# One ring tile for the split weights, with a fixed place for stationary operands, and a fourth buffer for raw weights

## The chip, the cores and the metric

The kernel runs on one core of a Trainium2 chip. The metric is device time in microseconds (us) of one execution. The kernel before took 2450.12 us, the median of 3 runs (2442.09 to 2450.7).

## The reference

One layer of a streaming encoder over 256 tokens of width 2048, in float32. Four sub-layers follow each other, each as x += post(f(pre(x))) with RMS norms:

```python
h = rmsnorm(x, n_ffn1_pre)                       # 1. SwiGLU FFN, 2048 -> 5504 -> 2048
x = x + 0.5 * rmsnorm((silu(h @ w_gate) * (h @ w_up)) @ w_down, n_ffn1_post)
proj = rmsnorm(x, n_mix_pre) @ w_in              # 2. two token mixers, gated
merged = gates[0] * mla_branch(proj) + gates[1] * rwkv7_branch(proj)
x = x + rmsnorm(merged @ w_o, n_mix_post)
x = x + rmsnorm(memory_xattn(rmsnorm(x, n_x_pre), mem), n_x_post)   # 3. over 256 memory tokens
# 4. a second SwiGLU FFN, as 1
```

Nearly all arithmetic is in products of the 256 token rows with float32 weight matrices, 437 MB of reads in all.

## The kernel before

**Split products.** TensorE multiplies float32 in a reduced format (float32r). So each operand is split into a high part, which is the value cast to that format, and a low part, the remainder, and a product is three products: high by high, high by low, low by high. For activations the two parts are tiles such as `hT` (the normed input, transposed; 16 blocks of 2048 bytes per partition, each with 256 high and 256 low elements), `mh` and `ml` (the FFN's hidden values), `oT`, `mT`, `zh`, `zl`. For weights they are made on the fly.

**Weight tiles.** All weights go through `weights` (L156 to L182), in tiles of up to 128 x 1024 elements (512 KB, laid out in memory so that one transfer brings one tile). Per tile: SP issues the load into a raw buffer (`wraw`, L176), ScalarE casts it into the high part (`whi`, L178), VectorE subtracts (`wlo`, L179), TensorE reads both. `wraw`, `whi` and `wlo` are pools of three buffers each. A raw buffer is free again when VectorE has read it; a `whi` buffer when TensorE's last matmul on it is done.

**Two kinds of product.** `lin_ch` (L188) makes channel-major results. The weights are the stationary operand, loaded into TensorE 128 columns at a time, and `hT` streams through: L196 multiplies a block of `whi` with the high and low half of `hT` at once (512 columns), L199 a block of `wlo` with the high half (256 columns). One tile of 1024 weight columns serves eight such pairs. `lin_tok` (L209) makes token-major results. The activations are stationary and the weights stream: L217 (high by `whi`), L218 (high by `wlo`), L219 (low by `whi`).

**Where the tiles lie.** In `lin_ch` the tile is not at the start of its buffer: a counter `turn` shifts it by (L165)

```python
a, b = 32 * (self.turn % 4), 32 * (self.turn // 4 % 4)
```

elements of 4 bytes, `a` in `whi` and `b` in `wlo`. In `lin_tok` both are 0. The buffers are 4608 bytes apart (9 x 512), and as built, `hT` starts at byte 50688 of each partition, the first `whi` buffer at 95744 and the first `wlo` buffer at 109568; each is a multiple of 512 bytes away from `hT`.

**Which product comes when.** Tiles in the order of the code: FFN1 gate and up (172, `lin_ch`), w_down (88, `lin_tok`), the latents of w_in (14, `lin_tok`), the low-rank columns of w_in (4, `lin_ch`), the v columns (16, `lin_tok`), w_ukv and w_uq (12, `lin_tok`), r and k columns of the first head group (16, `lin_ch`), w_oa (16, `lin_tok`), r and k of the second group (16, `lin_ch`), the gates (64), w_ob (16) and w_o (32, all `lin_tok`), then w_ckv in turns of 4 `lin_ch` and 4 `lin_tok` tiles, three times; four `lin_ch` products with w_cq (16); the fourth turn of w_ckv (4 and 4); w_co (16, `lin_tok`); FFN2 as FFN1.

**Feeds.** For FFN1 and for the memory tokens, `hT` itself is made from a raw buffer: `feed` (L335 to L340) loads a transposed block of x or mem (`in_xT`, `in_memT`) into a `wraw` buffer and splits it. There the three raw buffers hold activations and weights by turns. In FFN1's first column group the gate and up products advance in step, four blocks of `hT` at a time. x itself is loaded after the last split of the feed (L1113), for the row norms; their reciprocal roots are spread over a tile by L259.

**Order of the work.** A scheduler in the tile library orders the instructions of each engine by the order of the code and by priorities (the casts stand 100 places ahead, L177), and sets the waits between engines from the bytes that each instruction reads and writes. Every engine works its own list in order.

Of the kernel before, what the change touches and what calls it, by code (L numbers as in the profile page):

```python
# [18 lines left out]
P = 128  # L19
# [5 lines left out]
KF = DFF // P  # L25
EPS = 1e-6
WT = 1024
SKEW = 4
LEAD = 100

# [46 lines left out]
class Layer:  # L77
    def __init__(self, ctx, tc, a):
        self.ctx, self.tc, self.nc, self.a = ctx, tc, tc.nc, a
        nc = self.nc  # L80
        mk = lambda n, b, **k: ctx.enter_context(tc.tile_pool(name=n, bufs=b, **k))
        self.const = mk("const", 1)
        self.hpool = mk("hpool", 2)
        self.dram = mk("dram", 1, space=bass.MemoryType.DRAM)
        self.wraw = mk("wraw", 3)
        self.whi = mk("whi", 3)
        self.wlo = mk("wlo", 3)
        self.tmp = mk("tmp", 1)
        self.stat = mk("stat", 4)
        self.gp = mk("gp", 2)  # L90
        self.psm = mk("psm", 4, space=PSUM)
        self.pst = mk("pst", 2, space=PSUM)
        self.pss = mk("pss", 2, space=PSUM)

        self.ident = self.const.tile([P, P], F32, tag="ident", name="ident")
        make_identity(nc, self.ident)
        self.cols = self.const.tile([P, NCOL], F32, tag="cols", name="cols")
        nc.scalar.dma_start(out=self.cols, in_=a["cols"])
        self.inv = self.const.tile([P, 32], F32, tag="inv", name="inv")
        nc.scalar.dma_start(out=self.inv, in_=a["inv"])  # L100
        self.mhalf = self.const.tile([P, 1], F32, tag="mhalf", name="mhalf")
        nc.gpsimd.memset(self.mhalf, -0.5)

        self.pad(self.const, 128)
        warm = self.const.tile([P, 1], F32, tag="warm", name="warm")
        nc.scalar.activation(out=warm, in_=self.mhalf, func=AF.Copy, scale=self.mhalf)
        self.pad(self.gp, 64)
        self.lead = LEAD
        self.turn = 0
        self.X = self.hpool.tile([P, NT, D], F32, tag="big", name="X")  # L110

    def pad(self, pool, n):
# [43 lines left out]
    def weights(self, w, nk, c0, n, feed=None, still=False):  # L156
# [3 lines left out]
        for k in range(0, nk, kt):  # L160
            m = min(kt, nk - k)
            raw = self.wraw.tile([P, WT], F32, tag="wraw", name="wraw")
            a = b = 0
            if still:
                a, b = 32 * (self.turn % 4), 32 * (self.turn // 4 % 4)  # L165
                self.turn += 1
            hi = self.whi.tile([P, WT + 128], F32R, tag="whi", name="whi")[:, a : a + WT]
            lo = self.wlo.tile([P, WT + 128], F32R, tag="wlo", name="wlo")[:, b : b + WT]
            o = P * (nk * c0 + k * n)
            src = w[o : o + P * m * n].rearrange("(p x) -> p x", p=P)  # L170
            step = 1 if k == 0 and feed is not None else m
            for j in range(0, m, step):
                if feed is not None:
                    feed(k + j, step)
                e = slice(j * n, (j + step) * n)
                nc.sync.dma_start(out=raw[:, e], in_=src[:, e])  # L176
                with self.ahead(self.lead):  # L177
                    nc.scalar.copy(out=hi[:, e], in_=raw[:, e])  # L178
                    self.last_split = nc.vector.tensor_sub(  # L179
                        out=lo[:, e], in0=raw[:, e], in1=hi[:, e].bitcast(F32))  # L180
                for i in range(j, j + step):
                    yield k + i, hi[:, i * n : (i + 1) * n], lo[:, i * n : (i + 1) * n]  # L182
# [1021 lines left out]
```

## Time and profile before

| | before |
|---|---|
| median of 3 runs | 2450.12 us (2442.09 to 2450.7) |
| the profiled execution | 2451.06 us |
| its span, first to last instruction | 2449.3 us |
| mean granted TensorE clock | 0.99 |
| TensorE busy (PE) | 2391.3 us, 98% |
| VectorE busy (DVE) | 1489.7 us, 61% |
| ScalarE busy (ACT) | 1146.5 us, 47% |
| DMA | 450.36 MB, 184 GB/s |

PE is TensorE's matmul side, PEld its loading of stationary operands, which overlaps with PE. Busy times are between an instruction's modelled start and end, and matmuls overlap each other, so how fast TensorE goes is read from the starts of successive matmuls. SPq is SP's queue, which issues the loads.

### The profile page before, as it was taken

The page shows a single profiled execution, that of the slowest core. Times are in us where ns is not written, and L with a number is a line of the kernel's source. Part 1 is how long each engine was busy: PE and PEld are TensorE (multiplying, and loading weights), DVE is VectorE, ACT ScalarE, POOL GpSimd, SP SyncE. Part 2 cuts the span into 40 slices and gives each one's busy share as a digit, 9 for nine tenths or more (in the row PEclk, how much of TensorE's full clock was granted, in tenths as well). Part 3 has the DMA queues.
Part 4 walks back from the last instruction along what each step waited for, and adds up shares of the span by engine and source line. Part 5 has one row for each costly group of instructions (what it writes and reads, how often), then busy time and mean ns, then how long its engine had stood idle before and what let it go on. Part 6 is the DMA issues. An engine that isn't in the chain of part 4 may idle for free.

```text
span 2449.3 us, 33193 instructions
## 1 busy us (share of the span) xinstructions
PE 2391.3 (98%) x12682; PEld 2023.3 (83%) x12682; DVE 1489.7 (61%) x2262; ACT 1146.5 (47%) x1700; POOL 88.1 (4%) x126
## 2 busy tenths in 40 slices
PE   8999999999999999999999999999999999999997
PEld 6888888888888877887877677987888888888886
DVE  5666666654447566774873757555666666664444
ACT  6444444444446455443432446445554444444443
POOL 0000000000000102002011100000000000000000
PEclk9999999999999999999999999999999999999999
DMA  6555555556666644453653676545455555565664
GB/s 229 193 187 187 188 188 189 189 194 198 198 195 208 208 145 138 147 179 99 182 190 120 205 247 200 187 147 189 162 187 188 187 189 189 189 197 188 203 197 152
DMA packets 138719, 450.36 MB, mean 184 GB/s; under 512 B 24000, under 2 KB 26560, under 8 KB 138304
## 3 DMA queue, kind: packets, MB, share of 16 engines
q1 hardware_dynamic: 132896, 434.17, 54.6%
q0 software_dynamic: 4944, 13.64, 1.9%
q8 instruction: 99, 1.62, 0.3%
q10 hardware_dynamic: 720, 0.44, 0.1%
q14 instruction: 60, 0.49, 0.1%
HBM read 437.69 MB, written 10.49 MB: 183 GB/s over the span
## 4 chain that ended last, share of the span: by engine, by line
PE 87%; DMA 4%; DVE 4%; issue 2%; ACT 2%; POOL 1%; SPq 0%; DVEq 0%; ACTq 0%; POOLq 0%
PE mm L196 30%; PE mm L199 16%; PE mm L219 12%; PE mm L218 11%; PE mm L217 11%; DVE wlo L179 2%; PE po L847 1%; ACT whi L178 1%; PE po L848 1%; PE gr L802 1%; PE pn L860 1%; DMA ov<-osc 0%; DMA wraw<-in_xT 0%; PE po L869 0%; DMA wraw<-in_w_o 0%
## 5 line engine op out<-in xcount | busy, mean ns | idle before, releaser
L179 DVE TENSOR_TENSOR wlo<-wraw,whi 128x1024 fp32r<-128x1024 f32 (+2 forms) x796 | 960.1, 1207 | 724.1 <-ACT whi L178 715.6
L178 ACT CAST whi<-wraw 128x1024 fp32r<-128x1024 f32 (+2 forms) x796 | 826.1, 1038 | 921.2 <-PE mm L219 448.2
L196 PE MATMUL mm<-hT,whi 128*128 128x512 f32 x3296 | 1159.4, 396 | 8.1 <-DVE hT L288 5.6
L199 PE MATMUL mm<-hT,wlo 128*128 128x256 f32 x3296 | 916.1, 284 | 3.1 <-DVE wlo L179 3.1
L196 PEld LDWEIGHTS mm<-hT,whi 128*128 128x128 f32 x3296 | 615.5, 189 | 143.4 <-ACT whi L178 9.2
L199 PEld LDWEIGHTS mm<-hT,wlo 128*128 128x128 f32 x3296 | 622.9, 189 | 18.5 <-DVE wlo L179 6.4
L219 PE MATMUL mm<-whi,ml 128*128 128x512 f32 x688 | 267.7, 389 | 0.0
L218 PE MATMUL mm<-wlo,mh 128*128 128x512 f32 x688 | 267.7, 389 | 0.0
L217 PE MATMUL mm<-whi,mh 128*128 128x512 f32 x688 | 267.6, 389 | 0.0
L218 PE MATMUL mm<-wlo,hT 128*128 128x512 f32 (+2 forms) x512 | 187.4, 366 | 2.7 <-DVE wlo L179 2.7
L217 PE MATMUL mm<-whi,hT 128*128 128x512 f32 (+2 forms) x512 | 187.5, 366 | 0.5 <-ACT hT L287 0.5
L219 PE MATMUL mm<-whi,hT 128*128 128x512 f32 (+2 forms) x512 | 187.6, 367 | 0.0
L218 PEld LDWEIGHTS mm<-wlo,mh 128*128 128x128 f32 x688 | 129.1, 188 | 27.1
L217 PEld LDWEIGHTS mm<-whi,mh 128*128 128x128 f32 x688 | 129.1, 188 | 26.9
L219 PEld LDWEIGHTS mm<-whi,ml 128*128 128x128 f32 x688 | 129.1, 188 | 26.4
L205 ACT COPY half<-mm 128x256 f32<-128x256 f32 x206 | 75.6, 368 | 141.7 <-PE mm L196 141.7
L206 DVE TENSOR_TENSOR half<-half,mm 128x256 f32<-128x256 f32 x206 | 85.7, 417 | 56.9 <-ACT half L205 56.9
L218 PEld LDWEIGHTS mm<-wlo,hT 128*128 128x128 f32 x512 | 97.4, 190 | 18.1 <-DVE wlo L179 4.0
L217 PEld LDWEIGHTS mm<-whi,hT 128*128 128x128 f32 x512 | 97.4, 190 | 14.7 <-ACT hT L287 0.8
L219 PEld LDWEIGHTS mm<-whi,hT 128*128 128x128 f32 x512 | 97.0, 190 | 14.8 <-issue 1.0
L251 POOL TENSOR_TENSOR rstd<-rstd,mhalf 128x1 f32<-128x1 f32 x22 | 14.1, 644 | 1827.9 <-DVE rstd L249 1791.3
L218 PE MATMUL mm<-wlo,mT 128*128 128x512 f32 x128 | 50.8, 397 | 0.5 <-DVE wlo L179 0.5
(276 smaller groups left out, 1900.4 us busy)
## 6 DMA issues: line engine op xcount, KB each, us to landing
wraw<-in_w_ffn_up SPq DMA_DIRECT2D x172, 512.0 KB, 4.1
wraw<-in_w_ffn_gate SPq DMA_DIRECT2D x171, 512.0 KB, 4.2
wraw<-in_w_ffn_down SPq DMA_DIRECT2D x168, 512.0 KB, 4.2
wraw<-in_w_in SPq DMA_DIRECT2D x124, 512.0 KB, 3.4
wraw<-in_w_o SPq DMA_DIRECT2D x32, 512.0 KB, 3.3
wraw<-in_w_ckv SPq DMA_DIRECT2D x31, 512.0 KB, 3.4
wraw<-in_w_oa SPq DMA_DIRECT2D x16, 512.0 KB, 3.3
wraw<-in_w_ob SPq DMA_DIRECT2D x16, 512.0 KB, 4.7
```

Of the source, the lines that this page charges most:

```text
L178: nc.scalar.copy(out=hi[:, e], in_=raw[:, e])
L179: self.last_split = nc.vector.tensor_sub(out=lo[:, e], in0=raw[:, e], in1=hi[:, e].bitcast(F32))
L196: both = lambda: nc.tensor.matmul(ps[j], hi[:, s], x[:, k], start=(k == 0), stop=(k == nk - 1))
L199: nc.tensor.matmul(ps[j][:, 0, :], lo[:, s], x[:, k, 0], start=False, stop=False)
L205: nc.scalar.copy(out=y, in_=ps[j][:, 1, :])
L206: nc.vector.tensor_add(y, y, ps[j][:, 0, :])
L217: nc.tensor.matmul(ps[t], xh[:, k, s], hi, start=(k == 0), stop=False)
L218: nc.tensor.matmul(ps[t], xh[:, k, s], lo, start=False, stop=False)
L219: self.last_mm = nc.tensor.matmul(ps[t], xl[:, k, s], hi, start=False, stop=(k == nk - 1))
L802: nc.tensor.matmul(ps[:, p, :], self.bk[:, c, p, :], self.ar[:, c, p, :], start=True, stop=True)
L847: nc.tensor.matmul(po[:, p, :], self.ar[:, c, p, :], S[:, p, :], start=(p == 0), stop=False)
L848: nc.tensor.matmul(po[:64, p, :], G[64:, c, p, :64], self.uv[64:, c, p, :], start=(S is None and p == 0), stop=(p == GP - 1))
```

## The change

The two pools of three buffers for the split weights become one tile each, `whi` and `wlo`, used as a ring of three slots of 1024 elements. `turn` now counts every weight tile, modulo 3, and picks the slot. In `lin_ch` a tile lies at a fixed 64 elements (256 bytes) past the start of its slot in `whi` and 32 elements (128 bytes) in `wlo`; in `lin_tok` at the start of the slot. So a `lin_ch` tile reaches 64 (32) elements into the slot behind; behind the third slot these elements are spare. The raw weights get four buffers instead of three. The pools of scratch tiles stand in another order, and as built `whi` lies at byte 123904 and `wlo` at 99840, with `hT` at 50688 as before; xattn's own `hT` at 136704. Lines below L27 move down by two, lines between the constructor and `weights` by four, those behind L168 by one.

```diff
 WT = 1024
+RING = 3
+STILL = (64, 32)
 SKEW = 4
...
-        self.wraw = mk("wraw", 3)
-        self.whi = mk("whi", 3)
-        self.wlo = mk("wlo", 3)
+        self.wraw = mk("wraw", 4)
+        self.lo_pool = mk("lo", 1)
+        self.stat = mk("stat", 4)
         self.tmp = mk("tmp", 1)
-        self.stat = mk("stat", 4)
         self.gp = mk("gp", 2)
+        self.hi_pool = mk("hi", 1)
...
-        self.pad(self.gp, 64)
         self.lead = LEAD
         self.turn = 0
+        self.whi = self.hi_pool.tile([P, RING * WT + STILL[0]], F32R, tag="whi", name="whi")
+        self.pad(self.hi_pool, 512 - 4 * STILL[0])
+        self.wlo = self.lo_pool.tile([P, RING * WT + STILL[1]], F32R, tag="wlo", name="wlo")
...
             raw = self.wraw.tile([P, WT], F32, tag="wraw", name="wraw")
-            a = b = 0
-            if still:
-                a, b = 32 * (self.turn % 4), 32 * (self.turn // 4 % 4)
-                self.turn += 1
-            hi = self.whi.tile([P, WT + 128], F32R, tag="whi", name="whi")[:, a : a + WT]
-            lo = self.wlo.tile([P, WT + 128], F32R, tag="wlo", name="wlo")[:, b : b + WT]
+            a, b = (WT * self.turn + x for x in (STILL if still else (0, 0)))
+            self.turn = (self.turn + 1) % RING
+            hi, lo = self.whi[:, a : a + WT], self.wlo[:, b : b + WT]
```

The same instructions run, on all engines; some stand elsewhere in their engine's list. ScalarE where FFN1 passes from w_up to w_down, in the kernel before (4607 is the raw buffer of the last tile of w_up, 4642 of the first of w_down, 4660 of its second; the names in brackets are the semaphores waited for):

```order
L178 CAST whi_4608<-wraw_4607 128x1024 [waits DMAHW3_49,PE_49,Activation_49]
L284 CAST mh_110<-sg_4426 128x256 [waits DVE_49]
L178 CAST whi_4643<-wraw_4642 128x1024 [waits DMAHW4_49,PE_49,Activation_49]
L205 COPY half_4577<-mm_4532 128x256
L178 CAST whi_4661<-wraw_4660 128x1024 [waits DMAHW5_49,PE_49,Activation_49]
L404 ACTIVATE sg_4580<-sg_4580 128x256 [waits DVE_49]
```

and there in the changed kernel (4267 is the last tile of w_up, 4300 the first of w_down, 4316 and 4332 its second and third):

```order
L179 CAST whi_104<-wraw_4267 128x1024 [waits DMAHW3_49,PE_49,Activation_49]
L285 CAST mh_112<-sg_4100 128x256 [waits DVE_49]
L206 COPY half_4239<-mm_4198 128x256 [waits PE_49]
L405 ACTIVATE sg_4242<-sg_4242 128x256 [waits DVE_49]
L179 CAST whi_104<-wraw_4316 128x1024 [waits DMAHW5_49,PE_49,Activation_49]
L179 CAST whi_104<-wraw_4300 128x1024 [waits DMAHW4_49,PE_49,Activation_49]
L179 CAST whi_104<-wraw_4332 128x1024 [waits DMAHW6_49]
```

The cast of w_down's first tile moved behind that of its second, and both behind the copies of the product before. TensorE at the same place, before:

```order
L199 MATMUL mm<-hT,wlo 128x256 x2
L196 MATMUL mm<-hT,whi 128x512
L217 MATMUL mm<-whi,mh 128x512 [waits Activation_49]
L218 MATMUL mm<-wlo,mh 128x512 [waits DVE_49]
L219 MATMUL mm<-whi,ml 128x512
L217 MATMUL mm<-whi,mh 128x512 [waits PE_49]
```

and in the changed kernel, there and, after the dots, at the first w_ckv product of the memory tokens:

```order
L200 MATMUL mm<-hT,wlo 128x256 x2
L197 MATMUL mm<-hT,whi 128x512
L218 MATMUL mm<-whi,mh 128x512 [waits Activation_49]
L218 MATMUL mm<-whi,mh 128x512 [waits PE_49]
L219 MATMUL mm<-wlo,mh 128x512 [waits DVE_49]
L220 MATMUL mm<-whi,ml 128x512
...
L318 MATMUL tr<-ident,X 128x128 x7
L218 MATMUL mm<-whi,hT 128x256 x2
L219 MATMUL mm<-wlo,hT 128x256
L220 MATMUL mm<-whi,hT 128x256
```

Two products with the high part now stand ahead of the first with the low part, and at w_ckv seven transposes ahead of both; before, that product followed its `lin_ch` directly. SP's list at the kernel's start, before:

```order
L337 DMA wraw<-in_xT 128x256
L176 DMA wraw<-in_w_ffn_gate 128x256 x3
L337 DMA wraw<-in_xT 128x256 [waits DMAHW1_49,DMAHW0_49,DVE_49]
L337 DMA wraw<-in_xT 128x256 [waits DMAHW4_49,DVE_49]
L176 DMA wraw<-in_w_ffn_up 128x1024 [waits DMAHW5_49,DMAHW6_49,DMAHW3_49,DMAHW7_49,DMAHW2_49,DVE_49]
```

and in the changed kernel:

```order
L338 DMA wraw<-in_xT 128x256
L177 DMA wraw<-in_w_ffn_gate 128x256
L338 DMA wraw<-in_xT 128x256
L177 DMA wraw<-in_w_ffn_gate 128x256
L177 DMA wraw<-in_w_ffn_gate 128x256 [waits DMAHW0_49]
L338 DMA wraw<-in_xT 128x256 [waits DMAHW1_49,DVE_49]
L177 DMA wraw<-in_w_ffn_up 128x1024 [waits DMAHW4_49,DMAHW2_49,DVE_49]
```

A third load of `in_xT` now stands among the gate's, without a wait for VectorE.

## Rows read from the trace of the kernel before

**Rows 1.** The page: busy times of the engines; the chain that ended last, by engine.

```profile
PE 2391.3 (98%) x12682; PEld 2023.3 (83%) x12682; DVE 1489.7 (61%) x2262; ACT 1146.5 (47%) x1700; POOL 88.1 (4%) x126
...
PE 87%; DMA 4%; DVE 4%; issue 2%; ACT 2%; POOL 1%; SPq 0%; DVEq 0%; ACTq 0%; POOLq 0%
```

**Rows 2.** Groups by shape, matmuls: count, busy us, mean ns; idle time before.

```profile
L196 PE MATMUL mm<-hT,whi 128*128 128x512 f32 x3296 | 1159.4, 396 | 8.1 <-DVE hT L288 5.6 <-ACT whi L178 1.9 <-DVE half L206 0.5
...
L199 PE MATMUL mm<-hT,wlo 128*128 128x256 f32 x3296 | 916.1, 284 | 3.1 <-DVE wlo L179 3.1
...
L217 PE MATMUL mm<-whi,mh 128*128 128x512 f32 x688 | 267.6, 389 | 0.0
```

**Rows 3.** Windows, L196 alone: stretch, length, PE (count), PEld (count), clock, DMA.

```profile
0.00:291.00 291.00, 275.46 (x777) 146.30 (x777) 0.99 0.60 198
```

**Rows 4.** Timeline of PE (start us, length): first matmuls of still tiles.

```profile
291.00 0.39 PE L196 MATMUL mm<-hT,whi 128*128 128x512 f32 x1
...
305.00 0.39 PE L196 MATMUL mm<-hT,whi 128*128 128x512 f32 x1
...
307.78 0.39 PE L196 MATMUL mm<-hT,whi 128*128 128x512 f32 x1
...
335.78 0.39 PE L196 MATMUL mm<-hT,whi 128*128 128x512 f32 x1
...
349.79 0.39 PE L196 MATMUL mm<-hT,whi 128*128 128x512 f32 x1
...
352.56 0.39 PE L196 MATMUL mm<-hT,whi 128*128 128x512 f32 x1
```

**Rows 5.** Groups by shape, the split of a weight tile on VectorE and ScalarE.

```profile
L179 DVE TENSOR_TENSOR wlo<-wraw,whi 128x1024 fp32r<-128x1024 f32 x766 | 937.6, 1224 | 705.2 <-ACT whi L178 696.7
...
L178 ACT CAST whi<-wraw 128x1024 fp32r<-128x1024 f32 x766 | 806.0, 1052 | 897.2 <-PE mm L219 430.8 <-PE mm L196 257.9 <-issue 148.9
```

**Rows 6.** Timeline near 11 and 592 us; in brackets idle time and releaser.

```profile
10.68 1.05 ACT L178 CAST whi<-wraw 128x1024 fp32r<-128x1024 f32 x1 [1.80 <-DMA wraw<-in_w_ffn_up]
...
11.78 0.50 PEld L196 LDWEIGHTS mm<-hT,whi 128*128 128x128 f32 x2 [1.19 <-ACT whi L178]
...
13.04 0.29 PEld L199 LDWEIGHTS mm<-hT,wlo 128*128 128x128 f32 x1 [0.76 <-DVE wlo L179]
...
591.69 0.39 PE L218 MATMUL mm<-wlo,mh 128*128 128x512 f32 x1
591.92 0.39 PE L219 MATMUL mm<-whi,ml 128*128 128x512 f32 x1
...
592.35 1.06 ACT L178 CAST whi<-wraw 128x1024 fp32r<-128x1024 f32 x1 [1.66 <-PE mm L219]
```

**Rows 7.** Windows around two waits of TensorE: PE, PEld, DVE, ACT, POOL, clock, DMA.

```profile
1338.00:1350.00 12.00, 10.42 (x41) 7.25 (x40) 7.78 (x12) 4.99 (x6) 2.02 (x2) 1.00 0.64 218
...
1380.00:1392.00 12.00, 10.00 (x42) 7.84 (x41) 7.95 (x11) 4.33 (x5) 0.00 (x0) 0.86 0.62 212
```

**Rows 8.** The start: window, two xT loads in SP's timeline, one wait of TensorE.

```profile
0.00:32.00 32.00, 25.74 (x111) 19.88 (x112) 16.69 (x27) 17.24 (x30) 0.74 (x7) 1.00 0.68 221
...
7.91 0.33 SPq L337 DMA_DIRECT2D wraw<-in_xT  x1
...
21.27 0.33 SPq L337 DMA_DIRECT2D wraw<-in_xT  x1
...
PE rB L259 <- POOL rstd L251: 3.5, 1, 3.5
```

**Rows 9.** The feed of memT: window, and one wait of ScalarE (total, times, longest).

```profile
1500.00:1522.00 22.00, 18.59 (x99) 14.83 (x98) 20.52 (x39) 17.47 (x41) 1.10 (x2) 1.00 0.68 226
...
ACT hT L287 <- DMA wraw<-in_memT: 2.8, 3, 1.0
```

## The prediction

> **What bounds the kernel now.** I read four views: the page, the groups by shape, the timeline of TensorE, the waits. The page shows TensorE busy for 2391.3 of 2449.3 us, and the chain that ended last lies on it for 87% [rows 1]. VectorE and ScalarE have slack, so only two things can move the end: the distance from one matmul's start to the next, and the places where TensorE waits. Of its matmuls, 3296 pairs have weights as the stationary operand (L196 with whi over 512 columns, L199 with wlo over 256); the others (L217 to L219) stream the weights [rows 2]. Each weight tile serves eight such pairs, so there are 3296 / 8 = 412 of these tiles ("still" tiles), and `turn` counts them from 0.
>
> **The offset term.** In the kernel before, tile number t lies 128 x (t % 4) bytes (whi) and 128 x (t // 4 % 4) bytes (wlo) past hT's place modulo 512, so its trace already holds all 16 combinations. The change keeps one of them, 256 and 128, which is t % 16 = 6. By 291.00 us, 776 matmuls of L196 have started and the 777th starts [rows 3], so tile 97 begins there. Tile 113 begins at 335.78: sixteen tiles, all combinations once, take 44.78 us, 2.799 each. Tile 102 (t % 16 = 6) takes 307.78 - 305.00 = 2.78 us, and tile 118, also 6, takes 352.56 - 349.79 = 2.77 us [rows 4]. No wait lies in these stretches. So a pair costs 349.8 ns on average and 346.9 ns at 256 and 128. Saving: 2.799 - 2.775 = 0.024 us a tile, times 412 = **-9.9 us**. Rounding of the starts (0.01 us) leaves -7 to -13. That this place is reached follows from the built addresses: hT at byte 50688 of a partition, whi at 123904, wlo at 99840, both a multiple of 512 from hT; xattn's own hT, at 136704, too. The streamed tiles had offset 0 and keep it, so L217 to L219 get no term.
>
> These rows say that the place of a stationary operand costs time. The Trainium skill says the opposite: SBUF — State Buffer, section "Who interferes with whom", gives PE two read ports, one for the moving operand and one for LDWEIGHTS, "independent", and has PE never wait on anyone. This case's trace disagrees (2.799 against 2.775 us); by the rule the term would be nil and the sum +2.2 us, which is a rival below.
>
> **The hand-over term.** A ring of three slots of 1024 elements takes the place of three separate buffers. A still tile in slot r ends 64 elements (32 in wlo) inside slot r + 1. When the next tile is a streamed one, at offset 0, its cast writes these elements, so it must wait until TensorE has read the last still tile whole. Before, it waited for the tile three back. This is a new wait. The order shows it: in the first FFN the cast of the second w_down tile now stands ahead of that of the first, which waits on PE, and TensorE takes both hi products (L218) before the first lo product (L219). Tiles counted in the order of the code, the product changes from lin_ch to lin_tok after 172, 278, 322, 354, 470, 478, 486, 510 and 702 tiles. The slot is this number modulo 3; slot 0 is clear of it, because slot 2's tail lies in the spare elements behind the ring. That leaves five places: 172 (w_down of FFN1), 278 (v projection), 322 (w_oa), 470 and 478 (w_ckv).
>
> Price of one: a cast of 1024 takes 1052 ns and its subtraction 1224 ns [rows 5]. The cast starts 592.35 - 591.92 = 0.43 us after the start of the last matmul that it waits for, and where TensorE waited for a fresh tile in the start phase, the load of the lo operand came 13.04 - 10.68 = 2.36 us after the cast's start [rows 6]. So the first lo matmul starts 2.79 us after the last still matmul instead of three places later (3 x 0.23 = 0.69): 2.1 us. At 172, 278 and 322 nothing longer than two small transposes stands between, and I take 2.1 each. At 470 and 478 seven or more transposes of 128 columns do (the order shows them at 470): 0 to 2.1 each. I take half, since seven of them are about as long as one of the two pieces that the wait is made of. Sum 3 x 2.1 + 2 x 1.05 = **+8.4 us**, bounds 4 and 10.5. Queued behind the waiting cast on ScalarE are the next cast and the copies of the last lin_ch result; they would have waited for the same matmuls anyway.
>
> A halved clock could follow. With 1.6 us of idle TensorE in 12 us around 1343 the granted clock stayed 1.00; with 2.0 us idle around 1385 it was 0.86, 28% of 12 us at 1.2 instead of 2.4 GHz, so 1.7 us lost [rows 7]. The new idle time comes in two pieces of about 1.3 and 0.8 us, so it is nearer to the first row, and I take nothing; the bound is three times 1.7 = 5 us.
>
> **The fourth raw buffer.** In steady state ScalarE waits for TensorE to free whi, not for weights, so nothing is gained there. It matters where hT itself is built from raw buffers. At the start, loads of xT are issued at 7.91 and, two further on, at 21.27: 6.7 us for a group of three buffers (xT, gate, up), each released by VectorE before the next load [rows 8]. TensorE's work on a group is 16 pairs x 0.35 = 5.6 us. With four buffers the same latency gives 6.7 x 3/4 = 5.0 us, under 5.6, so TensorE sets the pace: 1.1 us saved in each of three groups. The third xT load now stands ahead of two gate pieces on SP's queue and no longer waits for VectorE, so the first up tile finds its buffer sooner; TensorE's weight load waited 1.19 us for that tile's cast [rows 6], of which I count 0.9. Sum 3 x 1.1 + 0.9 = **-4.2 us**. Bounds: 0, if transfers share the same rate; -6.3, all TensorE time not busy in the first 32 us (32 - 25.74). The wait for the row of rstd behind it (3.5 us, L259 [rows 8]) moves with it, since x is loaded after the last split of the feed.
>
> The feed of memT in xattn is the same thing once more: TensorE is idle for 22 - 18.59 = 3.4 us there, and ScalarE waits 2.8 us for memT [rows 9]. I take -2, bounds 0 and -3.4.
>
> **Edits that I cost at nothing.** The pools stat, tmp and gp move; only VectorE, ScalarE and GpSimd touch them, and their waits are covered by TensorE's 98%. Without that cover, L179's own idle time would have to be gone first. The scheduler's other reorderings are swaps of near neighbours; I allow 3 us either way in the range.
>
> **Sum.** -9.9 + 8.4 - 4.2 - 2 = -7.7 us. Against the profiled execution's 2451.06 us (span 2449.3) that is 2443.4; the median of the runs shown, 2450.12, is 0.9 below that execution, so the forecast for a median is 2442.4 us.
>
> **Rivals.**
> 1. *The hand-overs are hidden.* The cast may start sooner than its place in ScalarE's order says, or the fourth buffer fills the time. For it: at two places transposes already stand between. Against it: the cast's wait on PE is in the order, and a cast and a subtraction in series have a measured length. Then -9.9 - 4.2 - 2 = -16.1: 2434 us. Chance 0.22.
> 2. *The fourth buffer gives nothing.* At the start the 16 DMA engines are busy 0.68 of the time [rows 8], and more transfers in flight could each take longer. Then -9.9 + 8.4 = -1.5: 2448.6 us. Chance 0.20.
> 3. *Slower: the hand-over costs the clock as well.* Mechanism: TensorE idles at the five places, and its clock falls to half after each. Price 2.1 + 1.7 = 3.8 us each, 19 us in all, with the offset term kept and the buffer term lost: -9.9 + 19 = +9.1, 2459 us. It decides once a hand-over costs over (9.9 + 6.2) / 5 = 3.2 us with the buffer term, 2.0 without. Against it: the row at 1343 [rows 7]. Chance 0.08.
> 4. *The place of the operand costs nothing after all*, the difference between tiles having another cause. Then 8.4 - 6.2 = +2.2: 2452.3 us. The two tiles that agree speak against it [rows 4]. Chance 0.03. It is what the page SBUF — State Buffer of the Trainium skill would have.
>
> **How the numbers follow.** The forecast has 0.47. Its own range, from the bounds of its terms, is 2436 to 2450. A measurement of this kernel cannot tell changes under 0.5%, 12.3 us, from none: faster means under 2437.9, slower over 2462.4. Rival 1 lies mostly under it (0.16 of 0.22), and the forecast's lower tail adds 0.09: faster 0.25. Slower: half of rival 3 and a rest, 0.05. Same 0.70. For 8 in 10 the range takes in rival 2 and most of rival 1, and leaves out the ends of 1 and 3: 2433 to 2455.
>
> **What will show it.** In the timeline every still tile without a wait takes 2.77 to 2.78 us; if tiles still differ, the offset term is wrong. TensorE shows a wait of about 1.3 us for whi and then 0.8 us for wlo at the first w_down, v and w_oa products; if not, rival 1. The granted clock stays 1.00 there; if not, rival 3. At the start xT loads follow at 5.6 us instead of 6.7, and the row of rstd comes about 4 us earlier; if they do not, rival 2.

## The result, and the profile after

The changed kernel took 2435.64 us, the median of 16 runs (2428.35 to 2445.38), against 2450.45 us for the kernel before in 16 runs beside it. The ratio is 0.9944, with a 95% interval of 0.9928 to 0.9960, so about 14 us less. A second set of four runs (below) gave 2428.82 us and 0.9908 (0.9894 to 0.9923). The forecast was 2442.4 us, the range 2433 to 2455. Both kernels vary by some 8 us either way from run to run; most of it is clock, as shown below.

The profiled execution of the changed kernel took 2441.6 us, with a span of 2439.8 us, at a mean granted clock of 0.986 (before: 2451.06 us at 0.990). In the lines shown here every line number is one higher than before. First the page's busy times and the chain that ended last, which answer to [rows 1]:

```profile
PE 2385.9 (98%) x12682; PEld 2021.7 (83%) x12682; DVE 1487.9 (61%) x2262; ACT 1144.7 (47%) x1700; POOL 85.9 (4%) x126
...
PE 91%; DVE 4%; DMA 2%; issue 1%; ACT 1%; POOL 1%; SPq 0%; DVEq 0%; ACTq 0%; POOLq 0%
```

The chain now lies on TensorE for 91% instead of 87%, and on DMA for 2% instead of 4%. Something that had waited for transfers no longer does; this is the first sign of what the forecast missed.

The groups by shape (count | busy us, mean ns of one | idle time before, and what ended it), as [rows 2]:

```profile
L197 PE MATMUL mm<-hT,whi 128*128 128x512 f32 x3296 | 1146.9, 394 | 8.9 <-DVE hT L289 6.1 <-ACT whi L179 1.9 <-DVE half L207 0.8
L200 PE MATMUL mm<-hT,wlo 128*128 128x256 f32 x3296 | 912.4, 282 | 1.9 <-DVE wlo L180 1.9
...
L218 PE MATMUL mm<-whi,mh 128*128 128x512 f32 x688 | 267.6, 389 | 1.2 <-ACT whi L179 1.2
```

The still products are 2 ns shorter each, and the streamed one is unchanged, but now waits for a cast. In TensorE's timeline (start us, length) these are starts of L197 eight pairs, one still tile, apart, as [rows 4]:

```profile
185.72 0.39 PE L197 MATMUL mm<-hT,whi 128*128 128x512 f32 x1
...
188.49 0.39 PE L197 MATMUL mm<-hT,whi 128*128 128x512 f32 x1
```

2.77 us, and so for every still tile without a wait. Counted over all starts without one, a pair fell from 349.99 to 347.01 ns.

The first w_down product, where a streamed tile follows a still one, in the timeline (in brackets idle time and releaser):

```profile
492.08 2.00 ACT L179 CAST whi<-wraw 128x1024 fp32r<-128x1024 f32 x2 [1.85 <-PE mm L197]
493.15 2.36 DVE L180 TENSOR_TENSOR wlo<-wraw,whi 128x1024 fp32r<-128x1024 f32 x2 [1.67 <-ACT whi L179]
...
493.17 0.73 PE L218 MATMUL mm<-whi,mh 128*128 128x512 f32 x2 [1.18 <-ACT whi L179]
...
494.43 0.50 PE L219 MATMUL mm<-wlo,mh 128*128 128x512 f32 x1 [0.53 <-DVE wlo L180]
```

The cast starts only when the last still matmul has read its tile; TensorE waits 1.18 us for whi, takes the two hi products, and waits 0.53 us more for wlo. Windows (stretch, length, busy time and count of PE, PEld, DVE, ACT, POOL, then granted clock and DMA) at the start, at this place, at the same kind of place before w_oa, and at the feed of memT, as [rows 7 to 9]:

```profile
0.00:32.00 32.00, 24.42 (x126) 20.34 (x127) 17.95 (x28) 19.35 (x33) 0.74 (x7) 1.00 0.78 266
488.00:500.00 12.00, 10.29 (x50) 8.18 (x49) 6.42 (x8) 5.21 (x8) 0.00 (x0) 1.00 0.60 208
936.00:948.00 12.00, 10.02 (x31) 6.19 (x31) 7.18 (x12) 6.87 (x14) 8.39 (x7) 0.86 0.73 212
1494.00:1516.00 22.00, 19.21 (x101) 15.96 (x100) 19.67 (x36) 17.97 (x39) 1.10 (x2) 0.93 0.80 266
```

At w_down the clock stays 1.00. Before w_oa, with 2 us without a busy TensorE, it is 0.86, so 28% of these 12 us ran at 1.2 GHz. At the feed of memT TensorE isn't busy for 2.8 us of 22, it was 3.4; 1.9 of the 2.8 are the waits of the w_ckv product behind it, and the 0.93 is half clock behind that product. At the start TensorE has begun 126 matmuls by 32 us, before it were 111. The clock column says 1.00 there, but it counts the time ahead of the profile's first record of the clock as full. The starts say otherwise. Before, pairs stand 0.64 us apart up to 15.6 us:

```profile
14.28 0.63 PE L196 MATMUL mm<-hT,whi 128*128 128x512 f32 x1
...
14.92 0.63 PE L196 MATMUL mm<-hT,whi 128*128 128x512 f32 x1
```

That is the pace of 43.5 to 45.4 us too, where the recorded clock is 0.50; from 16 us on it is 0.36. In the changed kernel pairs stand 0.64 us apart only up to 7.3 us, in its second trace up to 9.3. So part of the gain at the start is a clock that rose sooner. SP's timeline has the last two loads of xT in the changed kernel:

```profile
11.29 0.33 SPq L338 DMA_DIRECT2D wraw<-in_xT  x1
...
17.17 0.33 SPq L338 DMA_DIRECT2D wraw<-in_xT  x1
```

They follow at 5.9 us, where it was 6.7. The wait for the row of rstd is 2.3 us instead of 3.5 [rows 8] (3.5 again in the second trace), and its first matmul starts at 39.6 instead of 42.8 us (39.5 in the second).

**Where the time came from.** The n-th matmul of one trace can be set against the n-th of the other. The table holds how much the difference (after less before, us) grows in stretches of the program; the last column is the changed kernel's second trace.

| stretch (us in the trace before) | first trace | second trace |
|---|---|---|
| start, to 49 | -5.1 | -2.8 |
| still tiles of FFN1, 49 to 495 | -4.2 | -4.2 |
| first w_down product, 495 to 504 | +2.3 | +2.3 |
| first v product, 784 to 796 | +1.9 | +1.9 |
| w_ukv, 814 to 838 | -2.8 | -2.7 |
| w_uq, 848 to 867 | -7.3 | -6.2 |
| w_oa and what runs beside it, 914 to 986 | +3.6 | +3.6 |
| 1114 to 1146 | +7.1 | 0.0 |
| 1273 to 1304 | +6.8 | -0.5 |
| 1367 to 1419 | -7.8 | -8.0 |
| feed of memT, 1487 to 1510 | -2.0 | -2.1 |
| first w_ckv products, 1510 to 1525 | +2.8 | +1.4 |
| still tiles of FFN2, 1734 to 2188 | -4.2 | -4.2 |
| whole | -9.5 | -23.5 |

Gains of 2.8, 7.3 and 7.8 us stand at places for which the forecast had nothing (2.7 and 2.6 of the last two came in e1 below as well, with neither ring nor fourth buffer; e2 shows the half clock in them), and the two traces of the same kernel differ by 14 us, nearly all of it at two places.

### The profile page after: what moved, and what is told of

Same layout as the page of the kernel before. It is cut to its first block, busy times and chain, and to the rows that moved or that the text cites. A ratio compares the mean times of both kernels' runs of the same rounds, so it can differ in the third digit from the quotient of the medians.

```text
span 2439.8 us, 33193 instructions
## 1 busy us (share of the span) xinstructions
PE 2385.9 (98%) x12682; PEld 2021.7 (83%) x12682; DVE 1487.9 (61%) x2262; ACT 1144.7 (47%) x1700; POOL 85.9 (4%) x126
## 4 chain that ended last, share of the span: by engine, by line
PE 91%; DVE 4%; DMA 2%; issue 1%; ACT 1%; POOL 1%; SPq 0%; DVEq 0%; ACTq 0%; POOLq 0%
PE mm L197 30%; PE mm L200 15%; PE mm L219 13%; PE mm L220 13%; PE mm L218 13%; DVE wlo L180 2%; PE po L848 1%; PE po L849 1%; PE gr L803 1%; PE pn L861 1%; ACT whi L179 1%; DMA ov<-osc 0%; PE lora L713 0%; PE po L870 0%; DVE X L387 0%
## 5 line engine op out<-in xcount | busy, mean ns | idle before, releaser
L197 PE MATMUL mm<-hT,whi 128*128 128x512 f32 x3296 | 1146.9, 394 | 8.9 <-DVE hT L289 6.1
L197 PEld LDWEIGHTS mm<-hT,whi 128*128 128x128 f32 x3296 | 613.6, 188 | 137.8 <-ACT whi L179 7.1
L218 PE MATMUL mm<-whi,mh 128*128 128x512 f32 x688 | 267.6, 389 | 1.2 <-ACT whi L179 1.2
L219 PE MATMUL mm<-wlo,mh 128*128 128x512 f32 x688 | 267.8, 389 | 0.5 <-DVE wlo L180 0.5
L220 PE MATMUL mm<-whi,ml 128*128 128x512 f32 x688 | 267.7, 389 | 0.0
L219 PE MATMUL mm<-wlo,hT 128*128 128x512 f32 (+2 forms) x512 | 190.8, 373 | 3.9 <-DVE wlo L180 3.9
L218 PE MATMUL mm<-whi,hT 128*128 128x512 f32 (+2 forms) x512 | 190.3, 373 | 1.9 <-ACT whi L179 1.7
L220 PE MATMUL mm<-whi,hT 128*128 128x512 f32 (+2 forms) x512 | 190.2, 372 | 0.0
L218 PEld LDWEIGHTS mm<-whi,mh 128*128 128x128 f32 x688 | 129.1, 188 | 28.1 <-ACT whi L179 1.5
L219 PEld LDWEIGHTS mm<-wlo,mh 128*128 128x128 f32 x688 | 129.2, 188 | 27.9 <-DVE wlo L180 1.0
L220 PEld LDWEIGHTS mm<-whi,ml 128*128 128x128 f32 x688 | 129.2, 188 | 26.7
L219 PEld LDWEIGHTS mm<-wlo,hT 128*128 128x128 f32 x512 | 99.2, 194 | 20.1 <-DVE wlo L180 5.2
L218 PEld LDWEIGHTS mm<-whi,hT 128*128 128x128 f32 x512 | 99.0, 194 | 17.7 <-ACT whi L179 2.3
L220 PEld LDWEIGHTS mm<-whi,hT 128*128 128x128 f32 x512 | 99.2, 194 | 15.5 <-issue 1.6
L218 PE MATMUL mm<-whi,oT 128*128 128x512 f32 x128 | 51.4, 403 | 1.4 <-ACT whi L179 1.4
```

Of the source, the lines that this page charges most:

```text
L197: both = lambda: nc.tensor.matmul(ps[j], hi[:, s], x[:, k], start=(k == 0), stop=(k == nk - 1))
L218: nc.tensor.matmul(ps[t], xh[:, k, s], hi, start=(k == 0), stop=False)
L219: nc.tensor.matmul(ps[t], xh[:, k, s], lo, start=False, stop=False)
L220: self.last_mm = nc.tensor.matmul(ps[t], xl[:, k, s], hi, start=False, stop=(k == nk - 1))
```

## Experiments

Two figures help to read them. One is the median with its ratio to the kernel before. The other is the mean time multiplied by the mean granted clock, what a run would take if all of its cycles came at the full 2.4 GHz; the rest, called clock loss here, is a measure of what half clock cost. It is no exact one: TensorE also idles at half clock, as behind its last matmul, and the start ahead of the first record is left out. Over the 16 runs of the changed kernel the time rises by 0.83 us for each us of it (correlation 0.94), and the spread (standard deviation) falls from 5.1 to 2.0 us when it is taken off. The four sets of the kernel before, on two chips, give 2421.8 to 2422.6 us at full clock, so kernels of different sets can be compared by it; with 4 to 20 runs a mean is uncertain by 0.5 to 1.1 us (standard error).

| kernel | runs | median | ratio (95%) | mean x clock | clock loss |
|---|---|---|---|---|---|
| before (four sets) | 59 | 2447.9 to 2452.1 | 1 | 2422.3 | 27.6 |
| changed | 16 | 2435.64 | 0.9944 (0.9928-0.9960) | 2408.7 | 27.0 |
| changed again, e8 | 4 | 2428.82 | 0.9908 (0.9894-0.9923) | 2411.2 | 17.6 |
| e1 place only | 6 | 2437.40 | 0.9946 (0.9924-0.9967) | 2413.5 | 23.2 |
| e2 three raw buffers | 12 | 2459.60 | 1.0025 (1.0007-1.0044) | 2423.4 | 33.6 |
| e3 no overlap | 4 | 2427.31 | 0.9905 (0.9886-0.9924) | 2405.0 | 23.1 |
| e11 no overlap again | 6 | 2429.40 | 0.9929 (0.9906-0.9952) | 2406.5 | 23.5 |
| e4 place zero | 6 | 2435.86 | 0.9941 (0.9922-0.9960) | 2417.3 | 19.5 |
| e5 whi 64, wlo 0 | 6 | 2444.40 | 0.9966 (0.9954-0.9979) | 2416.6 | 26.9 |
| e7 the same, three raw | 8 | 2460.77 | 1.0038 (1.0025-1.0051) | 2429.2 | 31.4 |
| e6 no pad of constants | 6 | 2433.49 | 0.9925 (0.9908-0.9942) | 2411.0 | 22.3 |
| e9 no overlap, mh moved | 6 | 2429.17 | 0.9919 (0.9893-0.9945) | 2406.5 | 22.7 |
| e10 overlap in wlo alone | 5 | 2424.40 | 0.9897 (0.9878-0.9916) | 2403.0 | 20.8 |
| e12 place mixed | 12 | 2457.07 | 1.0039 (1.0019-1.0058) | 2428.6 | 29.3 |

### e1: the place alone

```diff
-                a, b = 32 * (self.turn % 4), 32 * (self.turn // 4 % 4)
-                self.turn += 1
+                a, b = 64, 32
```

> The kernel before, with its three buffers each, but every still weight tile at 64 (whi) and 32 (wlo) elements, 256 and 128 bytes, instead of the rotation over 16 places; no ring, no fourth raw buffer, no reordered pools. Theory (the place sets the pitch of the pairs): the pair of L196 and L199 falls from 349.9 to 347.0 ns on average, 3296 x 2.9 ns = 9.6 us, about 2441 us, ratio to before 0.996; the still tiles all take 2.77 to 2.78 us. Rival (the place costs nothing, the gain came with the ring, the buffers or the pools): ratio 1.000, 2450 us.

At full clock it saves 8.3 us against the kernel before of its own set (2421.8), with 9.6 expected; in the trace the two FFNs' still tiles give 4.2 us each, as in the changed kernel. The median gains 14.7, because clock loss was smaller too (23.2 against 28.8). The rival falls: the place by itself carries this term.

### e2: three raw buffers

```diff
-        self.wraw = mk("wraw", 4)
+        self.wraw = mk("wraw", 3)
```

> The changed kernel with three raw buffers instead of four, all else kept. Theory (the fourth buffer is worth 5 us at the start, as the difference of the two traces shows, and up to 2 us at the feed of memT): 2441 to 2443 us, 5 to 7 above the changed kernel, ratio to before 0.997. Rival (the buffer gives nothing on the whole, since later waits take it back): as the changed kernel, 2435.6 us, ratio 0.994. Second rival (the part of the measured gain that the start, the still tiles and the hand-overs do not account for, some 4 to 6 us, also hangs on the buffer): 2446 to 2448 us, ratio 0.999.

All three were too low. Without the fourth buffer the changed kernel is slower than the kernel before: 24 us above the changed kernel, 14.7 of them at full clock. The waits say where. Waits of ScalarE's cast for a weight load (total us, times, longest), first in the kernel before:

```profile
ACT whi L178 <- DMA wraw<-in_w_in: 11.2, 4, 5.3
...
ACT whi L178 <- DMA wraw<-in_w_uq: 6.1, 2, 4.0
...
ACT whi L178 <- DMA wraw<-in_w_ukv: 5.4, 2, 4.5
...
ACT whi L178 <- DMA wraw<-in_w_ob: 3.8, 3, 2.5
```

In the changed kernel there are hardly any but at the start and in the FFNs:

```profile
ACT whi L179 <- DMA wraw<-in_w_ffn_gate: 4.3, 2, 3.0
...
ACT whi L179 <- DMA wraw<-in_w_ffn_up: 2.8, 3, 1.5
...
ACT whi L179 <- DMA wraw<-in_w_ukv: 1.9, 1, 1.9
```

With three buffers they are back:

```profile
ACT whi L179 <- DMA wraw<-in_w_in: 10.5, 3, 4.6
...
ACT whi L179 <- DMA wraw<-in_w_ob: 6.2, 3, 3.9
...
ACT whi L179 <- DMA wraw<-in_w_ukv: 5.3, 2, 4.5
...
ACT whi L179 <- DMA wraw<-in_w_uq: 5.0, 2, 3.7
```

All such waits together make 43 us in the kernel before, 9.5 in the changed one, 46 here. Timelines of the kernel before, VectorE and then ScalarE, show what stood behind the gains at 814 to 867:

```profile
825.83 0.69 DVE L676 TENSOR_TENSOR vp<-vp,vc 128x512 f32<-128x512 f32 x1 [4.61 <-DMA vp<-vraw]
```

```profile
832.05 1.05 ACT L178 CAST whi<-wraw 128x1024 fp32r<-128x1024 f32 x1 [3.94 <-DVE vp L678]
837.58 1.06 ACT L178 CAST whi<-wraw 128x1024 fp32r<-128x1024 f32 x1 [4.48 <-DMA wraw<-in_w_ukv]
...
862.16 0.83 ACT L178 CAST whi<-wraw 128x768 fp32r<-128x768 f32 x1 [4.05 <-DMA wraw<-in_w_uq]
```

VectorE frees a raw buffer by its subtraction. There its queue held elementwise work (vp) that itself waited 4.61 us for a transfer, so a cast waited for VectorE, buffers came free late, and the casts of w_ukv and w_uq waited 4.48 and 4.05 us for their loads; then TensorE waited too (3.7 us for qn). With a fourth buffer the same two loads:

```profile
829.86 1.05 ACT L179 CAST whi<-wraw 128x1024 fp32r<-128x1024 f32 x1 [1.85 <-DMA wraw<-in_w_ukv]
...
848.75 0.83 ACT L179 CAST whi<-wraw 128x768 fp32r<-128x768 f32 x1 [0.15 <-PE mm L220]
```

One cast waits 1.85 us for its load, the other for TensorE alone. At the same matmuls e2 lacks 2.6 us of the changed kernel's gain at the start, 2.8 at w_ukv, 5.3 at w_uq, 4.3 in 1391 to 1419 and 3.0 at memT, 18.0 in all. The whole traces differ by 17.2, but not for these places alone: e2 also loses 4.2 us at w_oa and wins 5.5 between 1120 and 1150, mostly by half clock in one trace and not in the other.

Half clock went with the buffer at two places. Windows of TensorE around w_uq and around 1400 us, before and then at the same code in the changed kernel:

```profile
840.00:875.00 35.00, 30.18 (x179) 0.90 0.60 189
1380.00:1430.00 50.00, 44.99 (x188) 0.90 0.69 240
```

```profile
830.00:865.00 35.00, 35.00 (x228) 1.00 0.67 226
1355.00:1420.00 65.00, 60.91 (x278) 1.00 0.71 253
```

All five traces with three raw buffers (before, e1, e2, e7, e12) have 3.4 to 10.2 us at 1.2 GHz in each of these two stretches, and none of the nine with four has any. The trace before has 6.8 and 10.2, so up to 3.4 and 5.1 us of the 7.3 and 7.8 gained there are clock; e1, with 3.4 at each, gains some of that without the buffer.

### e3 and e11: no overlap

```diff
-            a, b = (WT * self.turn + x for x in (STILL if still else (0, 0)))
+            a, b = (WT * self.turn + x for x in STILL)
```

> The changed kernel with the streamed tiles of lin_tok at the same places in the ring as the still ones (64 and 32 elements on), so no tile reaches into the next slot and no hand-over waits. Theory (the hand-overs cost 1.4 to 2.8 us at each of five places, about 10 us, and the place of a moving operand costs nothing): 2427 us, ratio to before 0.990, the pitch of L218 to L220 stays at 226 to 227 ns. Rival 1 (the place matters for moving weights as for still ones): some 4000 streamed matmuls change by up to 2 ns each, up to 8 us to either side, and the pitch shows it. Rival 2 (the idle time of the hand-overs would be lost anyway, at the next wait): as the changed kernel, 2435.6 us, ratio 0.994.

> The kernel without overlap once more, beside the other two on one chip and for a second trace. Theory: 2425 to 2429 us, ratio 0.990, at full clock 2405 us, L219 at 395 ns. Rival (its few runs were lucky ones): as the changed kernel, 2429 to 2436 us.

2427.31 and 2429.40 us, as expected. The matmuls by shape, in e3:

```profile
L197 PE MATMUL mm<-hT,whi 128*128 128x512 f32 x3296 | 1149.5, 395 | 6.7 <-DVE hT L289 5.5 <-ACT whi L179 1.2
...
L219 PE MATMUL mm<-wlo,mh 128*128 128x512 f32 x688 | 271.8, 395 | 0.0
```

L219, where wlo streams from 128 bytes past mh's place, takes 395 ns instead of 389. Over all products streamed matmuls of 512 columns start 230.3 ns apart instead of 227.1, and in e11's trace the streamed stretches without a wait take 8 us more than in e8's, twice what I had counted on. At full clock the ten runs average 2405.9 us, 3.3 below the 2409.2 of the changed kernel's twenty; with those 8 the overlap costs 11 us (e10 below makes it 9). In the window before w_oa the clock is now whole, 1.00 instead of 0.86:

```profile
936.00:948.00 12.00, 11.89 (x48) 8.36 (x49) 6.68 (x11) 6.70 (x13) 9.34 (x7) 1.00 0.71 211
```

So the 3.6 us at w_oa held some half clock as well. In median the gain over the changed kernel isn't settled: 2427 to 2429 against 2429 to 2436.

### e4: place zero

```diff
+            a, b = (WT * self.turn + x for x in (0, 0))
```

> The changed kernel with every weight tile at offset 0 of its slot, still ones too: no overlap between slots, four raw buffers, but the place of still weights is hT's own modulo 512 bytes. Theory (place sets the pitch; hand-overs cost about 10 us): pairs at 352.5 instead of 347.0 ns, 3296 x 5.5 ns = +18 us, less 8 to 10 us of hand-overs: 2444 to 2446 us, ratio to before 0.997 to 0.998, every still tile 2.82 us. Rival 1 (place costs nothing): as the kernel without overlap, 2427 us. Rival 2 (the hand-overs cost nothing): 2453.7 us, ratio 1.001.

L197 takes 399 ns instead of 394 and a pair 352.9 instead of 347. At full clock 8.1 us above the changed kernel's twenty runs, with 8 to 10 expected. The median, 2435.86, is some 9 us lower than expected, as its clock loss is only 19.5. Rival 1 falls with the pitch, rival 2 with the time at full clock.

### e5 and e7: whi 64 on, wlo at 0, with four and three raw buffers

```diff
+            a, b = (WT * self.turn + x for x in (64, 0))
```

> The changed kernel with every weight tile, still or streamed, at one place of its slot: whi 64 elements on, wlo at 0. No tile reaches into the next slot, and the still pair lies at 256 and 0 bytes past hT, where the trace of the kernel before has 347.2 ns. Theory (the kernel without overlap lost 4.4 us on L219, 395 instead of 389 ns, because the streamed wlo lay 128 bytes on): L219 back at 389 ns, 0.2 ns x 3296 = 0.7 us lost on the still pairs, so 3.7 us under the kernel without overlap: 2423 to 2425 us, ratio to before 0.989. Rival (L219's pace has another cause): 2428 us and 395 ns.

2444.40 us: 20 us too low a forecast. L219 did fall back to 389 ns, but the still pairs rose to 352.9 ns:

```profile
L197 PE MATMUL mm<-hT,whi 128*128 128x512 f32 x3296 | 1164.6, 399 | 8.6 <-DVE hT L289 5.7 <-ACT whi L179 2.1 <-DVE half L207 0.8
```

The 347.2 ns of this place had been read from the kernel before, where places change from tile to tile. It didn't carry over (e12).

> The kernel with whi 64 elements on and wlo at 0 for all tiles, with three raw buffers instead of four: the fourth buffer's worth where no slot is overlapped. Theory (the buffer takes away waits of the cast for late weights in the mixing stage, at w_in, w_uq, w_ukv, w_ckv, w_ob and w_o, 15 us at full clock, and some 6 us of half clock behind these waits): 20 us above the version with four, 2444 us, ratio to before 0.997, and the cast waits for loads of these tensors again, 25 to 40 us in all. Rival 1 (the buffer is worth only the 6 us forecast for the start and the feed of memT, the rest of the 24 us hung on the overlap): 2430 us, ratio 0.991. Rival 2 (nothing without the overlap): 2424 us.

Against e5, the same kernel with four buffers, 16.4 us are lost, 12.6 of them at full clock, and the casts wait 37 us for loads instead of 12. The absolute time is wrong by e5's error; the difference bears out the theory (20) and neither rival (6 and 0). So the buffer's worth doesn't hang on the overlap.

### e6: distance or address

```diff
-        self.pad(self.const, 128)
```

> The changed kernel without the pad of 128 bytes behind the constants: every later tile, hT and the weight rings alike, lies 128 bytes lower, and their distances stay. Theory (what counts is the distance between the still weights and hT modulo 512 bytes): nothing changes, pairs at 347.0 ns, 2435.6 us, ratio to before 0.994. Rival (what counts is the address itself modulo 512 bytes): the still tiles now lie where 128 and 0 bytes lay before, 352.8 ns a pair: +19 us, 2455 us, ratio 1.002.

2433.49 us and pairs at 346.6 ns, as in the changed kernel (346.6 in the same stretch). Weights and hT lay 128 bytes lower together, and the pace didn't change, so the distance counts and not the address. The hand-overs are those of the changed kernel too, but here half clock followed the one at w_down, where both traces of the changed kernel have 1.00 after the same waits of 1.18 and 0.53 us (PE, PEld, DVE, ACT, POOL, clock, DMA):

```profile
488.00:500.00 12.00, 10.29 (x44) 8.03 (x43) 5.50 (x8) 4.92 (x7) 0.00 (x0) 0.86 0.60 207
```

### e8: the changed kernel again

> The changed kernel as it is, once more, beside the others on one chip and for a second trace. Theory (a run's time follows the granted clock: the stretches at half clock in the mixing stage come and go between runs of one kernel): median 2433 to 2438 us, ratio to before 0.994; this profiled run differs from the first (2441.6 us, clock 0.986) by what its stretches at half clock differ, and the rest of the two traces agrees within 2 us. Rival (other waits, as DMA transfers, make the spread): the granted clock is alike and the time differs all the same.

2428.82 us, 4 below the expected band, with a clock loss 9 us smaller. The two traces differ by 14.0 us, 7.1 and 7.3 at the two places of the table above. Windows of the first trace (PE alone, then granted clock and DMA):

```profile
1105.00:1120.00 15.00, 15.00 (x107) 1.00 0.22 73
1120.00:1150.00 30.00, 30.00 (x129) 0.72 0.24 73
1262.00:1292.00 30.00, 28.54 (x121) 0.60 0.34 111
```

The same stretches in the second:

```profile
1105.00:1120.00 15.00, 15.00 (x105) 1.00 0.24 80
1120.00:1150.00 30.00, 29.87 (x168) 1.00 0.33 103
1262.00:1292.00 30.00, 29.78 (x188) 0.92 0.29 97
```

From 1120 to 1150 the first runs at a mean clock of 0.72, the second at 1.00, both with a TensorE that was busy by its rows (whose ends are modelled) all through the 15 us ahead, with about as many matmuls. It differs at a hand-over as well, the first w_ckv product, in the first trace and then in the second:

```profile
1505.00:1520.00 15.00, 12.69 (x80) 0.89 0.72 242
```

```profile
1492.00:1507.00 15.00, 12.87 (x91) 1.00 0.71 245
```

The theory holds: what separates runs of one kernel is mostly stretches at 1.2 GHz.

### e9: mh moved

```diff
+            a, b = (WT * self.turn + x for x in STILL)
...
+            self.pad(hid, 128)
             mh = hid.tile([P, KF, T], F32R, tag="mh", name="mh")
```

> The kernel without overlap (all weight tiles 64 and 32 elements on), with a pad of 128 bytes ahead of mh, so that mh and ml lie at the same place modulo 512 as wlo, and whi 128 bytes past them. Theory (L219's 395 instead of 389 ns came from the streamed wlo lying 128 bytes past the still mh): L219 falls back to 389 ns, 4.4 us less, 2420 to 2424 us if L218 and L220 do not mind 128 bytes between whi and mh; if they mind it as L219 did, they rise to 395 ns, +8.8 us, and the whole is 4 us above the kernel without overlap, 2432 us. Rival (the pace of L219 has nothing to do with mh's place): 395 ns as before and 2427 to 2428 us.

```profile
L218 PE MATMUL mm<-whi,mh 128*128 128x512 f32 x688 | 270.4, 393 | 0.0
L220 PE MATMUL mm<-whi,ml 128*128 128x512 f32 x688 | 269.0, 391 | 0.0
L219 PE MATMUL mm<-wlo,mh 128*128 128x512 f32 x688 | 267.0, 388 | 0.0
```

L219 fell to 388 ns, as the theory has it, but L218 and L220 rose to 393 and 391. The sum of the three is 806.4 us, in e11 806.3, so nothing is gained: 2429.17 us.

### e10: overlap in wlo alone

```diff
+            a, b = (WT * self.turn + x for x in (STILL if still else (STILL[0], 0)))
```

> The changed kernel with streamed whi tiles at the still ones' place (64 elements on) and streamed wlo tiles at 0 as in the changed kernel: whi slots no longer overlap, only wlo's do, by 128 bytes. Theory (a hand-over costs a cast and a subtraction in series; now the cast is free of it and only the subtraction waits): TensorE shows no wait for whi and one for wlo of 0.7 to 1.1 us at the five places, 4 to 5 us in all instead of 8 to 10, without half clock behind; L219 stays at 389 ns; at full clock 2405 us, as the kernel without overlap, and 2425 to 2430 us in median, ratio 0.990. Rival (the subtraction alone keeps the wait as long, since the first lo product comes right behind): waits of 2 us as before, 2432 to 2436 us, ratio 0.993.

2424.40 us (2420.25 to 2427.40), the lowest median of all, though its interval overlaps those of e3 and e11, and 2403.0 at full clock. Its interval lies below that of the changed kernel's first set (0.9928 to 0.9960), but overlaps that of its second. TensorE's waits for streamed tiles, in the changed kernel and then here:

```profile
PE mm L219 <- DVE wlo L180: 6.1, 8, 1.9
...
PE mm L218 <- ACT whi L179: 4.3, 4, 1.4
```

```profile
PE mm L219 <- DVE wlo L180: 4.7, 7, 1.4
```

No wait for whi is left, and that for wlo is shorter. Of 10.4 us, 2.2 are there without any overlap (e11), so the overlap's waits fall from 8.2 to 2.5 us, less than the 4 to 5 expected. At full clock e10 stands 6.2 us under the changed kernel; with these 2.5 the overlap costs 8.7. Cast and subtraction in series were the price, and freeing the cast takes most of it away. One part of the theory failed: e10's trace has 3.4 us of half clock at 960, 24 us behind the hand-over at w_oa, where no four-buffer trace without overlap has any.

### e12: places mixed

```diff
-                a, b = 32 * (self.turn % 4), 32 * (self.turn // 4 % 4)
+                a, b = 64, 0 if self.turn % 4 else 32
```

> The kernel before, with its three buffers each and no ring, whi of every still tile at 256 bytes, wlo of one still tile in four at 128 bytes and of the other three at 0. In the kernel before, which rotates, tiles at 256 and 0 took 347.2 ns a pair; in the ring kernel where all tiles lie there they took 352.9. Theory (the pace is carried on from the tile before: a tile at 256 and 0 keeps the fast rhythm that it is handed, and keeps the slow one too): all tiles stay at about 347 ns, as with the place alone, 2437 us, ratio 0.995. Rival (256 and 0 is slow by itself wherever tiles follow one another without rotation): three tiles in four at 352.9, 3296 x 3/4 x 5.9 ns = +14.6 us above the place alone, 2451 us, ratio 1.000.

My theory falls. Tiles at 256 and 128 bytes took 348.3 ns a pair, those at 256 and 0 behind them 353.3: they don't keep the fast rhythm. 2457.07 us, at full clock 15.1 above e1, as the rival had it (14.6); the rest of the 19.7 in median is clock loss. But slow "by itself" isn't the whole of it either, since such tiles did take 347.2 in the kernel before, where a tile at 128 and 0 came ahead of them. The place counts together with what came before it; how stays open.

## Why the prediction came out as it did

The time lies in the range, 6.8 us under the forecast. The sum was nearer than its terms.

1. **Offset term, -9.9: right.** Still tiles take 2.77 us, a pair 347.0 ns; 3296 x 2.98 ns = 9.8 us in the trace, 8.3 in e1 alone at full clock. The reading behind it was riskier than I knew: that a tile's pace in the rotation carries over to a kernel where all tiles lie there held for 256 and 128 bytes and for 0 and 0 (352.5 and 352.9), but failed for 256 and 0 (347.2 and 352.9). The Trainium skill (SBUF — State Buffer, "Who interferes with whom") calls the two read ports of PE, for the moving operand and for LDWEIGHTS, independent. Read so that place costs nothing, it doesn't fit e4 against the changed kernel: 352.9 against 347 ns with nothing moved but the weights' places. Whether ports are the cause no run here shows.
2. **Hand-over term, +8.4: right, at the upper end of its bounds (4 to 10.5).** The places were those named, with waits for whi of 0.7 to 1.4 us and for wlo of 0.5 to 0.9. At full clock the overlap costs 9 to 11 us. The lower bound doesn't follow from the terms, which give 6.3 (3 x 2.1) with both w_ckv places at nothing. At w_ckv I had halved the price for the transposes between. Matmul by matmul, the five four-buffer kernels without overlap gain 2.0 to 2.2 us on the changed kernel's second trace at the first of the two products and 0.9 to 1.1 at the other. So the transposes hid nothing at one and half at the other.
3. **Clock drop, 0: half right.** It stayed 1.00 at w_down in both traces, as read from the row at 1343, but fell to 0.86 before w_oa in both, fell behind the first w_ckv product in one of them, and at w_down in e6. So rival 3's mechanism exists, at one or two of the five places in a trace and for 1.7 us each, not the 5 x 1.7 that rival took; waits as long at w_down left 1.00 twice and 0.86 once, so their length alone doesn't decide it. What I had not thought of is that clock loss, 18 to 34 us in the mean of a kernel's runs, moves between runs by as much as a term of the sum.
4. **Fourth raw buffer, -6.2: the step that failed.** It was the sentence "In steady state ScalarE waits for TensorE to free whi, not for weights, so nothing is gained there". It holds inside the FFNs, as at 592.35 [rows 6], not in the mixing stage: the cast's waits for w_in, w_uq, w_ukv and w_ob stood in the trace before, 26.5 us, and are in none of the prediction's rows. The start (-2.8 to -5.1, forecast -4.2) and memT (-2.0, forecast -2) came out near the forecast, the start partly by luck. TensorE's work on a group was put at 5.6 us, at full clock; before, up to 15.6 us, it was 16 x 0.64 = 10.2, and that trace's late clock rise is in the difference. Over all traces the matmul that stands at 75 us in the trace before comes at 72.5 to 75.1 with three raw buffers and at 68.0 to 72.0 with four, 3.5 us earlier in the mean. The whole buffer is worth 12.6 (e7 against e5) to 14.2 us (e2 against all twenty runs, 2423.4 less 2409.2) at full clock, and 16 to 24 us in median. Rival 2, that it gives nothing, was the wrong way round.
5. **Edits at nothing, 0 ± 3: right.** -8.3 + 9 to 11 - 12.6 to 14.2 makes -14 to -10 at full clock; measured is 2409.2 - 2422.3 = -13.1, so little is left for pools and order. e2 against e1 says the same: 9.9 us at full clock for ring, pools and order together, where the overlap alone takes 9 to 11.

So the forecast of -7.7 missed 6 to 8 us of the buffer's gain; at full clock the kernel gained 13.1, and in mean time (2434.3 in twenty runs against 2450.0 in 59) 15.7. Rival 1's time (2434) was nearly hit, for another reason: its mechanism, hidden hand-overs, isn't there.

## What to carry to other kernels

Ask for the waits of the engine that takes the loads, tensor by tensor over the whole program, before costing a buffer: a few stretches of 20 us held most of the gain here. Where slots of a ring overlap, the price is the chain of the writers (cast, then subtraction), so move the overlap to the last of them or take it away. A pace read from tiles that take turns may not hold when all tiles do the same, so try the fixed case by itself.

## Not expected of the hardware

- A pair's pace depends on the distance of still weights from the streamed operand modulo 512 bytes (346.6 at 256 and 128, 352.9 at 0 and 0, e6 against the address), and also on the tiles that came before (256 and 0: 347.2 or 352.9). It shows with streamed weights too: 389 ns at 0 bytes, 395 at 128 (L219).
- TensorE's clock halves in stretches of the mixing stage in some runs and not in others of one kernel (0.72 and 1.00 from 1120 to 1150), though TensorE was busy all the time ahead by its rows. At two stretches it went with the buffer instead: half clock in five of five traces with three raw buffers, in none of nine with four.
- The profile counts the time ahead of the clock's first record as full clock, though pairs there stand 0.64 us apart and not 0.35; here that hid 3 to 11 us of half clock at the start of a run.
